# Norms of a Hymba-style decoder step: the reciprocal root as one power on GpSimd, spread over the partitions by ones times diagonals

## The chip, the cores and the metric

The kernel runs on one core of one Trainium2 chip. The metric is the device time of one launch in microseconds (us). Engines are named as in the profile: PE is TensorE's matmul, PEld its weight load, DVE is VectorE, ACT is ScalarE, POOL is GpSimd, SP is SyncE, which issues most DMAs; SPq, POOLq and ACTq are their DMA queues. All arithmetic is float32. A tile of type `fp32r` holds float32 values that were rounded so that PE reads them in one pass; a plain float32 matmul takes two passes of PE (two matmul records each). Where the kernel wants float32 accuracy from the rounded type it splits a value into a high part (the value, rounded) and a low part (the rest), and adds two or three products.

## The reference, cut to what matters

One layer of a decoder is computed for 2048 new tokens (the prompt) and for 8 x 4 = 32 sample tokens, 2080 columns in all. Width is 1024, the feed-forward width 2816.

```python
def rmsnorm(x, g):
    y = x32 * lax.rsqrt(jnp.mean(x32 * x32, axis=-1, keepdims=True) + EPS)   # EPS = 1e-6
    return y * g

a = rmsnorm(x, norm_attn_g)
qa, fa, ia, ga, qb, kb, vb = split(a @ w_in)
o_a = rmsnorm(gla_chunked(q_a, k_a, v_a, log(forget), s0), hgrn_onorm_g) * silu(ga)   # per head, 128 wide
o_b = dilated_attn(q_b, k_b, v_b)
h = x + concat(o_a, o_b) @ w_o
hn = rmsnorm(h, norm_ffn_g)
h = h + (silu(conv(hn @ w_gate)) * (hn @ w_up)) @ w_down
h = h + sigmoid(rmsnorm(h, norm_ple_g) @ w_ple_gate) * (p @ w_ple_proj)
y = rmsnorm(h, norm_final_g)
```

So a token is normed five times, and each norm needs one number for a token, 1/sqrt(mean + EPS).

## The kernel before, in words

Activations lie with features on partitions and tokens along the free dimension. A norm therefore needs a sum over partitions and then the result on every partition. It is made in these steps:

- `rstd_cols`: PE multiplies the tile of squares `ssq` by a column of ones, 128 tokens at a time (L114), so that 128 tokens stand on 128 partitions and a norm over T tokens is a tile of 128 x ceil(T/128) numbers, `rs_v`. DVE scales and adds EPS (L121, L122).
- `rsqrt_small`: DVE takes the reciprocal root of that small tile, by a bit trick on integers (L100, L101) and three Newton steps of three instructions (L103, L104, L105): 11 instructions that each need the one before.
- `bcast_rows`: for every column of 128 tokens, PE multiplies the column, repeated 128 times as weights, by the identity `ident` (L129). That leaves each token's number on all 128 partitions, in PSUM. These are float32 matmuls, two passes each. `bcast_all` does so for four columns at a time, and ACT copies the result to SBUF (L138).

The program has four parts.

1. Projections of the first 1024 and then of the other 1056 tokens (`in_phase`, norms at L254 on chunks of 256 to 384 tokens). Next to the first half, `w_down` is combined and rounded for a Strassen product and written to DRAM. A projection's output is scaled with the token's norm `rb` when DVE empties PSUM (L300), or with the column `rc` or `rq` by ACT (L357).
2. Next to the second half, eight units of the HGRN recurrence (`hgrn_unit`). Each norms its output per head: sums of squares by ACT (L558), `o_v` (L561), `rsqrt_small` on 128 x 8 (L562), then DVE scales `at` (L567), PE turns it (L574) and DVE gates it (`hg`, L575).
3. Attention over the prompt. On PE the order of this part is written out by hand (the scheduler may not move its matmuls). Into it are woven the last HGRN unit, the attention of the sample tokens, whose cached keys and values are loaded as `skt`, and the recurrence of the sample tokens, which has one norm of its own (`hsv`, L660 and L661, scaled at L662, turned at L665). POOL takes part in the attention: keys and queries are prepared there (`kL`, `qS`), and the coefficients of the three dilations.
4. The trunk: three blocks of 696, 696 and 688 tokens, first through the output product (`out_block`), then all through the feed-forward (`ffn_block`), then all through the embedding gate (`embed_block`). The product of the Strassen scheme with `w_down` (`downs`) is done there too; its weights `w` come from DRAM `wd_d` by DMAs that POOL issues (L1275). There are eight norms of whole blocks: three before the feed-forward, three before the gate, and the final norms of blocks 0 and 1. Two more make the final norm of block 2 (`now`, in 432 and 256 tokens). The steps of a norm are not done at once: `rstd` hands back two functions, one for the sums and the root, one for the spreading, and they are called some matmuls apart, as `mid` inside `dense_first` or from the list `late`.

Outside of the attention on PE, a scheduler orders the instructions of every engine, by a model of its own of how long things take; each engine then works through its list in that order. So a change in one place can move instructions in others. The pool of wide tiles of the trunk, `w` from `wide`, has 44 buffers.

## Time and profile before

| what | value |
|---|---|
| median of 3 runs | 3017.25 us (3016.31 to 3018.32) |
| the profiled execution | 3014.84 us |
| its span, first to last instruction | 3013.0 us |
| granted TensorE clock, mean | 0.988 |
| PE busy | 2926.5 us, 97% of the span |
| DVE busy | 2191.6 us, 73% |
| ACT busy | 1304.5 us, 43% |
| POOL busy | 667.9 us, 22% |
| `rsqrt_small` | 25 calls, 275 instructions on DVE |
| spreading matmuls (L129) | 71, in 142 records |

The profiled execution took 2.4 us less than the median. An engine's busy time is the time in which it works on anything; matmuls overlap, so that PE can be busy without being at its peak. A row of a timeline gives the start in us, the length in us, engine, line, operation and out<-in, and in brackets how long the engine sat idle before it and what ended that. Rows of equal neighbours are merged (x4).

### The profile page before, as it was taken

How to read it: one execution, taken by the hardware profiler on the slowest of the kernel's cores; microseconds unless marked ns; L12 is line 12 of the kernel's file. 1: busy time of each engine (PE TensorE's matmuls, PEld its weight loads, DVE VectorE, ACT ScalarE, POOL GpSimd, SP SyncE). 2: the span in 40 equal slices, each digit the busy share in tenths (PEclk: the TensorE clock that was granted, in tenths of full speed). 3: DMA queues.
4: the chain of work that ended last, by engine and by line, in shares of the span. 5: the costliest groups of instructions: out<-in, count | busy, mean ns of one | idle time of the engine just before them, and what ended most of it. 6: DMA issues, size and time to landing. Idle time of an engine off the chain costs nothing.

```text
span 3013.0 us, 52001 instructions
## 1 busy us (share of the span) xinstructions
PE 2926.5 (97%) x18639; PEld 2738.0 (91%) x18639; DVE 2191.6 (73%) x4761; ACT 1304.5 (43%) x2824; POOL 667.9 (22%) x780
## 2 busy tenths in 40 slices
PE   8999999999978989999999999999999999999998
PEld 8977789987767667999999999999999999999997
DVE  7666868884466557568988889766769777777777
ACT  5333423231156665334444444544444544444443
POOL 1443222221134553102443431000001000000000
PEclk9999999999989999999999999999999999999999
DMA  5898533342248996766666568677778777778873
GB/s 174 311 337 309 198 103 110 104 134 95 91 115 243 303 246 194 260 225 222 227 209 194 191 198 300 231 250 252 245 231 311 242 245 244 257 248 290 272 274 131
DMA packets 328579, 664.08 MB, mean 220 GB/s; under 512 B 46400, under 2 KB 114112, under 8 KB 326528
## 3 DMA queue, kind: packets, MB, share of 16 engines
q1 hardware_dynamic: 291472, 472.65, 48.4%
q0 software_dynamic: 33264, 121.13, 12.6%
q10 hardware_dynamic: 3584, 66.98, 6.1%
q8 instruction: 147, 2.41, 0.3%
q14 instruction: 112, 0.92, 0.1%
HBM read 513.69 MB, written 213.92 MB: 241 GB/s over the span
## 4 chain that ended last, share of the span: by engine, by line
PE 72%; issue 9%; DVE 7%; DMA 7%; ACT 2%; POOL 2%; SPq 1%; DVEq 0%; POOLq 0%; ACTq 0%
PE mm L142 16%; PE mm L144 16%; PE mm L143 16%; PE mm L346 2%; PE mm L344 2%; PE mm L345 2%; PE lv L484 2%; PE acc L822 2%; PE S L797 1%; PE PT L810 1%; PE S L798 1%; DMA draw<-in_w_down_dram 1%; DMA xr<-in_xT_dram 1%; DVE h L1291 1%; DMA wd_d<-dw 1%
## 5 line engine op out<-in xcount | busy, mean ns | idle before, releaser
L143 PE MATMUL mm<-w 128*128 128x348 f32 (+3 forms) x3636 | 1166.1, 321 | 1.1 <-DVE w L1435 0.7
L142 PE MATMUL mm<-w 128*128 128x348 f32 (+3 forms) x3508 | 1109.7, 323 | 15.2 <-ACT s L1233 5.8
L144 PE MATMUL mm<-w 128*128 128x348 f32 (+3 forms) x3508 | 1117.4, 321 | 1.3 <-DVE w L181 1.3
L143 PEld LDWEIGHTS mm<-w 128*128 128x128 f32 x3636 | 684.3, 188 | 3.8 <-DVE w L1067 1.8
L142 PEld LDWEIGHTS mm<-w 128*128 128x128 f32 x3508 | 656.5, 188 | 23.6 <-ACT s L1233 8.5
L144 PEld LDWEIGHTS mm<-w 128*128 128x128 f32 x3508 | 659.0, 188 | 2.6 <-DVE w L181 1.8
L181 DVE TENSOR_TENSOR w<-raw,w 128x512 fp32r<-128x512 f32 x586 | 421.9, 725 | 170.3 <-ACT w L180 165.3
L180 ACT CAST w<-raw 128x512 fp32r<-128x512 f32 x586 | 360.6, 621 | 402.8 <-PE mm L144 293.1
L1275 POOL DMA_DIRECT2D w<-wd_d x231 | 123.8, 536 | 906.2 <-PE mm L144 800.6
L1291 DVE TENSOR_TENSOR h<-h,mm 128x348 f32<-128x348 f32 (+1 forms) x504 | 248.4, 509 | 45.9 <-PE mm L144 44.4
L803 ACT ACTIVATE P<-P,st 128x256 f32<-128x256 f32 (+3 forms) x256 | 134.1, 526 | 87.5 <-DVE st L802 85.9
L802 DVE CUSTOM_DVE_ANT_0 P<-S,mask 128x256 f32<-128x256 f32 (+3 forms) x256 | 105.0, 449 | 73.1 <-PE S L798 50.1
L1233 ACT COPY s<-mm 128x348 f32<-128x348 f32 (+1 forms) x198 | 87.9, 444 | 158.1 <-PE mm L144 157.8
L345 PE MATMUL mm<-wl,xh 128*128 128x512 f32 x352 | 140.7, 400 | 1.1 <-DVE wl L267 1.1
L344 PE MATMUL mm<-wh,xh 128*128 128x512 f32 x352 | 140.6, 403 | 0.0
L346 PE MATMUL mm<-wh,xl 128*128 128x512 f32 x352 | 140.3, 399 | 0.0
L142 PE MATMUL mm<-xh,wh 128*128 128x384 f32 (+2 forms) x384 | 125.7, 332 | 8.6 <-ACT xh L242 5.1
L143 PE MATMUL mm<-xl,wh 128*128 128x384 f32 (+2 forms) x384 | 126.9, 333 | 0.8 <-DVE xl L243 0.8
L144 PE MATMUL mm<-xh,wl 128*128 128x384 f32 (+2 forms) x384 | 125.5, 330 | 1.5 <-DVE wl L267 1.4
L267 DVE TENSOR_TENSOR wl<-wraw,wh 128x512 fp32r<-128x512 f32 x104 | 86.3, 851 | 34.0 <-POOL wh L148 28.9
L181 DVE TENSOR_TENSOR dw<-draw,dw 128x512 fp32r<-128x512 f32 x77 | 69.4, 909 | 55.8 <-ACT dw L180 55.0
L797 PE MATMUL S<-kH,qS 128*128 128x256 f32 (+3 forms) x256 | 97.7, 396 | 8.2 <-DVE st L802 7.3
(348 smaller groups left out, 5155.0 us busy)
## 6 DMA issues: line engine op xcount, KB each, us to landing
w<-wd_d POOLq DMA_DIRECT2D x231, 512.0 KB, 5.6
wd_d<-dw SPq DMA_DIRECT2D x77, 512.0 KB
out_sk_dram<-in_cache_k_dram ACTq DMA_DIRECT2D x56, 584.0 KB
out_sv_dram<-in_cache_v_dram ACTq DMA_DIRECT2D x56, 584.0 KB
raw<-in_w_gate_dram SPq DMA_DIRECT2D x110, 256.0 KB
raw<-in_w_up_dram SPq DMA_DIRECT2D x110, 256.0 KB
wraw<-in_w_in_dram SPq DMA_DIRECT2D x104, 256.0 KB
raw<-w_gate_d SPq DMA_DIRECT2D x88, 256.0 KB
```

Of the source, the lines that this page charges most:

```text
L142: PE.matmul(ps, lhsT=wh, rhs=xh, start=first, stop=False, skip_group_check=read)
L143: PE.matmul(ps, lhsT=wh, rhs=xl, start=False, stop=False, skip_group_check=read)
L144: PE.matmul(ps, lhsT=wl, rhs=xh, start=False, stop=last, skip_group_check=read)
L180: A.copy(w[:, 0], raw)
L181: V.tensor_sub(w[:, 1], raw, f32(w[:, 0]))
L344: PE.matmul(ps, lhsT=xh[k][:, js], rhs=wh, start=k == 0, stop=False)
L345: PE.matmul(ps, lhsT=xh[k][:, js], rhs=wl, start=False, stop=False)
L346: PE.matmul(ps, lhsT=xl[k][:, js], rhs=wh, start=False, stop=k == NK - 1)
L797: PE.matmul(s[:, w * i:w * i + w], lhsT=bl.q(hh), rhs=bl.k(kH, hh), start=True, stop=False)
L803: A.activation(pe, pe, AF.Exp, bias=mn, scale=-1.0, accum_out=st[:, bl.r, hh, 0:1])
L1275: G.dma_start(t, wd_d[p][n - 1])
L1291: V.tensor_add(o, o, acc[m][:, :H])
```

## The change: what it does

- `rsqrt_small` becomes one instruction on POOL: the tile to the power of -0.5, the exponent read from a constant 128 x 1 tile. This holds for all 25 calls.
- For the eight whole-block norms of the trunk, `bcast_split` replaces `bcast_all`. The column of roots is split into `rs_hi` (rounded) and `rs_lo` (the rest) on DVE. For each group of up to four columns, a 128 x 512 tile is filled with the identity, times the column, so that each 128 x 128 block has 128 tokens' numbers on its diagonal: POOL makes the one of the high part, DVE the one of the low part, into two more buffers of the pool of wide tiles. PE multiplies each by a matrix of ones, both into the same PSUM tile, with the rounded type. The copy by ACT stays.
- The norms in `in_phase` and in `now` keep the old spreading.
- The old tile of ones shrinks to two columns; a rounded 128 x 128 tile of ones comes beside it.

```diff
-    ones = const.tile([128, 128], F32, name="ones")
+    ones = const.tile([128, 2], F32, name="ones")
     V.memset(ones, 1.0)
+    ones_r = const.tile([128, 128], F32R, name="ones_r")
+    V.tensor_copy(ones_r, ones[:, 0:1].to_broadcast([128, 128]))
+    power = const.tile([128, 1], F32, name="power")
+    G.memset(power, -0.5)
...
     def rsqrt_small(pool, v, shape):
-        i = pool.tile(shape, I32, name="rs_i")
         y = pool.tile(shape, F32, name="rs_y")
-        t = pool.tile(shape, F32, name="rs_t")
-        V.tensor_scalar(i, v.bitcast(I32), 1, None, op0=ALU.logical_shift_right)
-        V.tensor_scalar(y.bitcast(I32), i, -1.0, RSQRT_SEED, op0=ALU.mult, op1=ALU.add)
-        for _ in range(3):
-            V.tensor_mul(t, y, y)
-            V.scalar_tensor_tensor(t, t, -0.5, v, op0=ALU.mult, op1=ALU.mult)
-            V.scalar_tensor_tensor(y, t, 1.5, y, op0=ALU.add, op1=ALU.mult)
+        G.tensor_tensor(y, v, power.to_broadcast(shape), op=ALU.pow)
         return y
...
+    def bcast_split(pool, wide, pps, cols, nt, T, dst, tag="ms"):
+
+        hi = pool.tile([128, nt], F32R, name="rs_hi")
+        lo = pool.tile([128, nt], F32R, name="rs_lo")
+        V.tensor_copy(hi, cols)
+        V.tensor_sub(lo, cols, f32(hi))
+        for j0 in range(0, nt, 4):
+            nj = min(4, nt - j0)
+            n = min(T, 128 * (j0 + nj)) - 128 * j0
+            eye = ident.rearrange("p (o t) -> p o t", o=1).to_broadcast([128, nj, 128])
+            ps = pps.tile([128, 512], F32, name=tag)
+            for x, (part, eng) in enumerate(((hi, G), (lo, V))):
+                d = wide(128 * nj, F32R)
+                col = f32(part)[:, j0:j0 + nj].rearrange("p (j o) -> p j o", o=1).to_broadcast([128, nj, 128])
+                eng.tensor_mul(d.rearrange("p (j t) -> p j t", t=128), eye, col)
+                PE.matmul(ps[:, :n], lhsT=ones_r, rhs=d[:, :n],
+                          start=x == 0, stop=x == 1)
+            A.copy(dst[:, 128 * j0:128 * j0 + n], ps[:, :n])
...
-        def rstd(ssq, T, c0=0, n=None):
+        def rstd(ssq, T, c0=0, n=None, split=True):
...
-                        lambda: bcast_all(pmm, rc[0], -(-n // 128), n, rb[:, c0:c0 + n], "mm"))
+                        lambda: (bcast_split if split else bcast_all)(*([sm, wide] if split else []), pmm, rc[0], -(-n // 128), n,
+                                                                  rb[:, c0:c0 + n], "mm"))
 
         def now(ssq, T, c0=0, n=None):
-            rb, steps = rstd(ssq, T, c0, n)
+            rb, steps = rstd(ssq, T, c0, n, False)
```

A source line of the changed kernel stands 15 or 16 lines lower from `bcast_all` on (L567 becomes L582, L802 L817, L1291 L1307), and `rsqrt_small`'s power is L101, the diagonals and their matmuls are L143 and L144.

Three places of the order that the engines' lists show. First, the last HGRN unit, inside the attention: DVE before, up to the scaling of `at`. `rs_t` and `rs_y` are the root's steps, `pt` copies of turned scores, `mn` a minimum for the attention's coefficients, `hg` the gated output:

```order
L812 COPY pt<-PT 128x512
L736 TENSOR_REDUCE mn<-st 128x8
L104 SCALAR_TENSOR_TENSOR rs_t<-rs_t,o_v 128x8
L105 SCALAR_TENSOR_TENSOR rs_y<-rs_t,rs_y 128x8
L103 TENSOR_TENSOR rs_t<-rs_y 128x8
L567 TENSOR_TENSOR at<-at,rs_y 128x512 x2
```

These are the last rows of a stretch that begins with `o_v` (L561): between it and L567 stand the root's eleven steps, six scores (L802), three copies `pt` (as one, one and one) and `mn`, mixed. DVE in the changed kernel at the same place:

```order
L576 TENSOR_SCALAR o_v<-o_ssq 128x8
L817 ISA P,st<-S,mask 128x256
L827 COPY pt<-PT 128x512
L827 COPY pt<-PT 128x512 x2
L751 TENSOR_REDUCE mn<-st 128x8
L582 TENSOR_TENSOR at<-at,rs_y 128x512 x2
```

(The score row comes six times.) The eleven steps are gone; the same scores and copies stay ahead of the scaling. The power is POOL's, in the midst of its work for the attention:

```order
L752 TENSOR_TENSOR w<-mn,st 128x16
L711 TENSOR_TENSOR kL<-stage,kH 128x4x128
L101 TENSOR_TENSOR rs_y<-o_v,power 128x8
L163 TENSOR_SCALAR qS<-stage 128x512 x2
L755 TENSOR_TENSOR wl<-w,st 128x16
```

It stands between the two `kL`, which follow each other before.

Second, the first of the gate's norms (block 0), where the last products of the feed-forward are still being added to `h` (L1291 before, L1307 now) and weights are split (L181, now L196). DVE before:

```order
L122 TENSOR_SCALAR rs_v<-mm 128x5
L1291 TENSOR_TENSOR h<-h,mm 128x344 x2
L100 TENSOR_SCALAR rs_i<-rs_v 128x6
L181 TENSOR_TENSOR w<-raw,w 128x512
L101 TENSOR_SCALAR rs_y<-rs_i 128x6
L103 TENSOR_TENSOR rs_t<-rs_y 128x6
```

and DVE in the changed kernel:

```order
L118 TENSOR_SCALAR rs_v<-mm 128x5
L1307 TENSOR_TENSOR h<-h,mm 128x344 x2
L196 TENSOR_TENSOR w<-raw,w 128x512
L133 CAST rs_hi<-rs_y 128x6
L116 MEMSET rs_v 128x6
L1307 TENSOR_TENSOR h<-h,mm 128x344
L134 TENSOR_TENSOR rs_lo<-rs_y,rs_hi 128x6
L143 TENSOR_TENSOR w<-c_ident,rs_lo 128x512
L1307 TENSOR_TENSOR h<-h,mm 128x344 x4
L143 TENSOR_TENSOR w<-c_ident,rs_lo 128x256
```

(L1307 x2 comes once more ahead of the CAST, and L196 and L1307 once more ahead of the first L143.) Two small steps and two products of 512 and 256 elements have taken the place of ten small steps, and the CAST waits for POOL.

Third, PE in the trunk. Between a norm's sums (L114, now L110) and its first spreading matmul the scheduler puts other matmuls. For the eight norms in order their number was 49, 50, 60, 93, 44, 72, 41 and 24; now it is 79, 81, 36, 27, 41, 96, 43 and 24. At the fourth, the gate's first norm, PE in the changed kernel, from the first spreading matmul (high part) to the second (low part); L157 to L159 are the three products of `mm3`, 344 tokens wide:

```order
L144 MATMUL mm<-w,ones_r 128x512
L157 MATMUL mm<-w 128x344
L158 MATMUL mm<-w 128x344
L159 MATMUL mm<-w 128x344
L144 MATMUL mm<-w,ones_r 128x512
```

Where one block of twelve passes stood (L129 x6), there are now four single passes, here three to nine other matmuls apart, so that PE can wait at four places.

More of the change, by code (lines that the diff above doesn't have):

```diff
@@ L29 @@
 BIG = 1e30
-RSQRT_SEED = float(0x5F3759DF)
 BLOCKS = ((0, 1024), (1024, 1056))
```

## The prediction

> **What bounds the kernel now.** I read the page's shares first, then the stages, then who PE waits for, then the rows around each of the 25 roots.
>
> ```profile
> PE 2926.5 (97%) x18639; PEld 2738.0 (91%) x18639; DVE 2191.6 (73%) x4761; ACT 1304.5 (43%) x2824; POOL 667.9 (22%) x780
> ```
>
> ```profile
> core 0: us, PE busy (x) PEld busy (x) DVE busy (x) ACT busy (x) POOL busy (x), PEclk, DMA share, GB/s
> 420.00:840.00 420.00, 414.63 (x2483) 367.61 (x2482) 286.29 (x823) 98.87 (x268) 94.26 (x113) 0.99 0.35 112
> 930.00:1060.00 130.00, 122.97 (x1058) 89.10 (x1053) 72.66 (x273) 84.30 (x254) 57.89 (x69) 0.97 1.04 297
> 1240.00:1380.00 140.00, 140.00 (x900) 139.94 (x899) 92.37 (x159) 51.11 (x81) 4.76 (x4) 1.00 0.73 253
> 1380.00:1500.00 120.00, 115.77 (x717) 113.84 (x716) 115.69 (x171) 64.62 (x118) 47.01 (x34) 0.99 0.61 210
> 1500.00:2280.00 780.00, 776.40 (x4860) 773.16 (x4859) 605.60 (x1021) 349.91 (x672) 166.75 (x196) 1.00 0.71 233
> 2280.00:2745.00 465.00, 460.09 (x2899) 456.64 (x2899) 356.95 (x694) 226.09 (x473) 44.45 (x84) 1.00 0.78 258
> ```
>
> PE is the bound nearly everywhere: 140.0 of 140 us at the trunk's start, 414.6 of 420 next to HGRN. So DVE work that goes away is worth nothing by itself (275 steps of some 0.16 us, 44 us, 1.5% of the span); it counts only where PE waits at a root, or where PE itself has less to do. A matmul of the trunk costs 140.0 / 900 = 0.156 us.
>
> **The change, part by part.**
>
> *The tail.* The last norm stands alone on the path:
>
> ```profile
> 3001.84 0.16 DVE L122 TENSOR_SCALAR rs_v<-mm 128x2 f32<-128x2 f32 x1 [0.70 <-PE mm L114]
> 3002.03 0.17 DVE L100 TENSOR_SCALAR rs_i<-rs_v 128x2 int32<-128x2 int32 x1
> ...
> 3004.01 0.16 DVE L105 SCALAR_TENSOR_TENSOR rs_y<-rs_t,rs_y 128x2 f32<-128x2 f32 x1
> 3004.22 1.22 PE L129 MATMUL mm<-c_ident,rs_y 128*128 128x128 f32 x4 [2.42 <-DVE rs_y L105]
> ```
>
> Eleven steps from 3002.03 to 3004.17, and PE 0.05 us later: 2.2 us from `rs_v` to PE. In their place come a hop to POOL, one power and a hop to PE. No row has a power. The nearest, POOL's smallest two-input instruction:
>
> ```profile
> L741 POOL TENSOR_TENSOR mn<-wl 128x8 f32<-128x8 f32 x16 | 3.2, 201 | 0.9
> L696 POOL TENSOR_TENSOR kL<-stage,kH 128x512 fp32r<-128x512 f32 x30 | 46.0, 1552 | 12.7 <-ACT kH L695 10.8 <-issue 1.9
> ```
>
> It takes 0.20 us with as many elements; a power is more arithmetic. Bounds: 0.20 below; above 1.55, POOL's product of 64 times as many elements. I take 0.4, near the lower end, since most of 0.20 us cannot be arithmetic on 8 elements a partition. With two hops of 0.1 that is 0.6 for 2.2: -1.6 us (-1.8 to -0.45).
>
> *The start.* The first chunk's root is worked off in 9 us, since DVE weaves it into loading x:
>
> ```profile
> 21.67 0.15 DVE L122 TENSOR_SCALAR rs_v<-ms 128x2 f32<-128x2 f32 x1
> 31.24 0.15 DVE L105 SCALAR_TENSOR_TENSOR rs_y<-rs_t,rs_y 128x2 f32<-128x2 f32 x1
> 33.71 0.35 ACT L138 COPY rb<-ms 128x256 f32<-128x256 f32 x1
> 34.97 0.44 PE L142 MATMUL mm<-xh,wh 128*128 128x384 f32 x1 [2.25 <-DVE ev L300]
> ```
>
> PE has all its PSUM tiles full and waits 2.25 us for evictions that need `rb`. POOL is free there; with a root at 22.5 `rb` comes long before 31, and the wait goes. What is late next is x (ACT and its loads), so I take -2.0 (-2.3 to 0). The other five roots of the projections end no wait of PE: 0, covered by PE's 414.6 of 420 us and the like; were the cover gone, each would give back at most such a wait. The seven HGRN roots next to the projections likewise: 0, with 3 us either way for a reordered PE.
>
> *The last HGRN unit.* Here PE's order is fixed, and DVE is late:
>
> ```profile
> 911.15 0.50 DVE L561 TENSOR_SCALAR o_v<-o_ssq 128x8 f32<-128x8 f32 x1
> 911.88 3.07 POOL L696 TENSOR_TENSOR kL<-stage,kH 128x512 fp32r<-128x512 f32 x2
> 913.52 1.47 DVE L101 TENSOR_SCALAR rs_y<-rs_i 128x8 int32<-128x8 int32 x1
> 915.46 0.88 PE L822 MATMUL acc<-pt,v 128*64 128x128 f32 x12
> 920.69 1.29 DVE L567 TENSOR_TENSOR at<-at,rs_y 128x512 f32<-128x512 f32 x2
> 921.44 1.12 PE L574 MATMUL s<-c_ident,at 128*128 128x128 f32 x4 [5.10 <-DVE at L567]
> ```
>
> The root spreads over 9.5 us; one of its steps takes 1.47 us beside POOL's `kL`. Of the 9.5, some 4.9 are `o_v`, scores and copies that stay. The power stands behind the first `kL`, 911.88 + 3.07 / 2 = 913.4, and is done by 914: DVE no longer waits for it when it reaches L567 at about 916 to 917. PE, done at 916.3, then waits 0 to 1 us for 5.1. The wait costs more than its length:
>
> ```profile
> 916.00:922.00 6.00, 0.90 (x11) 0.66 (x6) 5.82 (x21) 2.25 (x9) 4.12 (x7) 0.81 0.86 213
> 922.00:926.00 4.00, 4.00 (x21) 3.67 (x21) 3.24 (x13) 3.19 (x7) 1.96 (x4) 0.50 0.76 266
> ```
>
> After it the granted clock is 0.50 for 4 us, that is 2 us of work. So 4.1 + 2 = 6 here. Behind it lies the loading of the sample's keys (DMA share 1.04 from 930 to 1060), which starts when this unit ends and so moves too, but not for certain. I take -4.5 (-7.2 to 0).
>
> *The sample's norm.*
>
> ```profile
> PE s L665 <- DVE hso L662: 1.5, 1, 1.5
> ```
>
> The same pattern, POOL idle: -1.2 (-1.5 to 0).
>
> *The trunk, PE's own work.* Eight spreadings of twelve passes become four passes each:
>
> ```profile
> 1290.52 1.21 PE mm L114 x12
> 1299.71 1.34 PE mm L129 x12
> ```
>
> ```profile
> 199.80 0.40 PE L345 MATMUL mm<-wl,xh 128*128 128x512 f32 x1
> 201.19 0.39 PE L345 MATMUL mm<-wl,xh 128*128 128x512 f32 x1
> ```
>
> The first pair is of the chain, start and share: 1.34 us for twelve. The second is a run of one-pass matmuls 512 wide: six in 1.39 us, 0.232 each. One of 184 lies between a 2-wide one (1.21 / 12 = 0.10) and a 344-wide one (0.156): 0.11. New: 2 x 0.232 + 2 x 0.11 = 0.68. Gain 0.66 x 8 = -5.2 us (-5.3 to -4.6).
>
> *The trunk, new waits.* From the sums to PE it is now DVE, POOL, DVE, POOL and DVE side by side. The diagonals are two-input products of 512 and 256 elements. POOL's:
>
> ```profile
> 1359.23 1.28 POOL L168 TENSOR_TENSOR raw<-raw 128x512 f32<-128x512 f32 x1 [133.02 <-DMA h_d<-h]
> 1445.77 1.28 POOL L176 TENSOR_TENSOR raw<-raw 128x512 f32<-128x512 f32 x1 [4.46 <-DVE rs_t L104]
> 1445.78 1.29 DVE L105 SCALAR_TENSOR_TENSOR rs_y<-rs_t,rs_y 128x6 f32<-128x6 f32 x1
> ```
>
> 1.28 us, and a DVE step beside it that else takes 0.16 takes 1.29: each POOL product can hold DVE as long. DVE has room for that (357 of 465 us) except at the trunk's feed-forward start (115.7 of 120). The chain, at the gate's first norm:
>
> ```profile
> 2746.88 1.47 PE L114 MATMUL mm<-ones,w 128*128 128x2 f32 x12 [0.70 <-DVE w L1048]
> 2747.59 0.68 DVE L181 TENSOR_TENSOR w<-raw,w 128x512 fp32r<-128x512 f32 x1
> 2749.03 0.14 DVE L121 TENSOR_SCALAR rs_v<-mm 56x1 f32<-56x1 f32 x1
> 2749.17 0.94 DVE L1291 TENSOR_TENSOR h<-h,mm 128x344 f32<-128x344 f32 x2
> ```
>
> Sums end at 2748.35; `rs_v` starts 0.68 later and takes 0.2; hop and power 0.5, hop and rounding 0.3, POOL's product 1.3: 3.0 us. Ahead of the rounding stand four additions (0.47 each) and a split (0.68), 2.6 us, of which 0.6 passes while POOL works: 5.0 in all. PE has 27 matmuls for it, 27 x 0.156 = 4.2. So PE is short 0.8, and as much again for the low part, whose product stands behind another split and two additions. By the same count the others have 12.3, 12.6, 5.6, 6.4, 15.0, 43 x 0.194 = 8.3 and 24 x 0.194 = 4.7 us (0.156 scaled to 432 columns); only the last is as tight. POOL's queue holds no DMA that would be late there: it is idle for 235 us from 2742 on.
>
> ```profile
> 2977.78 1.38 POOL L1513 TENSOR_SCALAR w<-w,c_gains 128x256 f32<-128x256 f32 x2 [235.22 <-ACT w L1044]
> ```
>
> For the first three it shares POOL with the weights' sums, with 5.6 us and more. I take +2.5 (0 to +8, a microsecond a norm). The four more wide buffers of a norm I cost at nothing: 44 cover them; if not, a load of `h` is late once a block, which the +8 holds.
>
> *Sum:* -1.6 - 2.0 - 4.5 - 1.2 - 5.2 + 2.5 = -12.0. Adding the ends gives -18 to +3 apart from the reordering. The profiled execution took 3014.84 and its span 3013.0, so 1.8 us lie outside and stay: 3002.8 for such an execution. The runs' median is 3017.25, 2.4 above it, and I forecast on that scale: 3017.25 - 12.0 = 3005.
>
> **The rivals.**
>
> *The gains outside the trunk aren't kept.* For: DMA share 1.04 right behind the largest of them; a stage that waits for loads gives nothing for an earlier start. Against: those loads are let go by the same unit's end, and PE is busy 123.0 of 130 us. Price: without -4.5, -1.2 and half of -2.0 the sum is -5.3: 3012.
>
> *PE waits in the trunk at every norm.* For: four places to wait instead of one, and the low part's product far down DVE's list. Against: six of eight norms have 5.6 us or more. Price: +8 for +2.5: 3010.5.
>
> *The power is slow* (the other side). POOL's row tells nothing of a power's arithmetic. Should it take 4.7 us, three times POOL's slowest row, the chain in the trunk is 9.3 us: short by 5.1, 4.6, 3.7, 2.9 and 1.0 at the five tight norms, 17.3 in all, and DVE stands still meanwhile at the rounding; -5.2 + 17.3 + 0.6 for the low part = +13. The tail loses 2.7, the unit in the attention gains only 2.5, the start still 2: +11, 3028. It decides from about 2.8 us a power on, where the trunk's loss (some +6) and a tail of +0.8 eat the rest. The Trainium skill (GPSIMD Engine Reference, Instruction dispatch) says that the first call into freshly loaded code of this engine pays about 6 us with no instruction to be seen. If the power lay in other code than the sums and were loaded at each change, the same working with 6 us would give about +20; no run here shows such a load.
>
> *The scheduler's new order costs.* PE's list differs in hundreds of rows from 300 to 840 us; 5.4 us of PE idle there can grow as well as shrink. Price 3 either way.
>
> **How the numbers follow.** A measurement here tells 0.2%, 6.0 us, from no change. The forecast, with sums from -8 to -17: 0.55, all faster. Gains not kept: 0.19, all within 0.2% (-5.3). Waits at every norm: 0.10, near -6.7, half faster and half within 0.2%. Slow power: 0.10, all slower. A costly order: 0.06, of which 0.04 within 0.2% and 0.02 slower. Faster 0.55 + 0.05 = 0.60; same 0.19 + 0.05 + 0.04 = 0.28; slower 0.10 + 0.02 = 0.12. The range runs from 3000 (-17) to 3018: below it 0.07, above it the slow power and part of the order, 0.12. The forecast's own range is 3000 to 3009.
>
> **What would show it.** A power below 0.5 us in POOL's rows; no wait of L574's successor at about 915 and a clock of 1.0 behind it; the first eviction before 31 us; four one-pass matmuls for each trunk norm, about 0.7 us; waits for POOL's and DVE's diagonals of 0 to 2 us at the gate's first and last norms; 0.6 us from `rs_v` to PE at the end. Powers above 2 us, or waits of PE for `w` of L143 beyond 5 us together, would prove it wrong.

## The result and the profile after

Eight runs of the changed kernel took 3029.16 us in the median, eight of the kernel before 3017.78; the ratio is 1.0038, 95% interval 1.0025 to 1.0052. So the change is slower, by 8 to 16 us, where -12 was forecast. The execution that was profiled first (8514.88 us, counted in that median; the other seven have 3026.78) is of no use for reading: rows of 348-wide matmuls are 0.66 us long in the mean there, where the next trace has 0.32, and a run of the kernel before took 7258.4 us later, so this is no matter of the change. The trace after is therefore that of another execution, 3032.50 us, on a chip where the changed kernel took 3028.98 in the median and the kernel before 3019.57, ratio 1.0027 (1.0014 to 1.0040). Line numbers of the changed kernel are 15 to 16 higher from `bcast_all` on: L567 is now L582, L574 is L589, L1141 is L1157; the new spreading is L133 (rounding), L134 (low part), L143 (diagonals) and L144 (PE), `mm3` is L157 to L159.

The page of the changed kernel, shares, and its windows with the columns of the windows shown before:

```profile
PE 2928.3 (97%) x18575; PEld 2738.5 (90%) x18575; DVE 2166.9 (71%) x4519; ACT 1304.1 (43%) x2824; POOL 707.6 (23%) x822
```

```profile
420.00:840.00 420.00, 412.19 (x2475) 366.74 (x2473) 273.82 (x738) 99.08 (x266) 106.63 (x120) 0.99 0.36 111
930.00:1060.00 130.00, 117.38 (x988) 82.76 (x986) 66.03 (x247) 77.38 (x236) 53.45 (x67) 0.95 1.03 274
1240.00:1380.00 140.00, 140.00 (x891) 139.77 (x890) 83.47 (x135) 50.30 (x78) 12.62 (x11) 1.00 0.69 239
1380.00:1500.00 120.00, 110.49 (x645) 105.63 (x644) 108.59 (x151) 58.18 (x108) 38.81 (x29) 0.94 0.65 225
2280.00:2745.00 465.00, 460.33 (x2904) 457.23 (x2903) 351.83 (x694) 219.45 (x467) 44.98 (x85) 1.00 0.78 260
```

DVE lost 25 us of work, as it should, and POOL gained 40. The window to look at is 1380 to 1500: PE did 645 matmuls there where it did 717, and its clock fell from 0.99 to 0.94, while DVE did less than before. PE is short of work, and DVE isn't the reason. Between 930 and 1060 PE is busy 5.6 us less; 3.1 us less are seen there in `before_b`, a second trace of the kernel before.

The power by shapes, in the groups of POOL (mean ns of one behind the busy time):

```profile
L101 POOL TENSOR_TENSOR rs_y<-o_v,power 128x8 f32<-128x8 f32 x8 | 13.3, 1659 | 6.0 <-DVE o_v L576 5.9
L101 POOL TENSOR_TENSOR rs_y<-rs_v,power 128x6 f32<-128x6 f32 x8 | 12.6, 1576 | 301.9 <-DVE rs_v L118 301.9
L101 POOL TENSOR_TENSOR rs_y<-rs_v,power 128x2 f32<-128x2 f32 x2 | 1.7, 834 | 6.0 <-DVE rs_v L118 6.0
L101 POOL TENSOR_TENSOR rs_y<-hsv,power 128x1 f32<-128x1 f32 x1 | 0.6, 571 | 5.6 <-DVE hsv L675 5.6
```

It costs by elements: 0.57 us for one on a partition, 1.66 for eight, which is four times the 0.4 I took. It is still less than the eleven steps it replaces, and below the 2.8 us from which I said it decides.

The second trunk norm, ahead of the second block's feed-forward, in the timeline of the changed kernel (start, duration, engine, line, operation; in brackets idle time and what ended it):

```profile
1362.02 1.36 PE L110 MATMUL mm<-ones,w 128*128 128x2 f32 x12
...
1364.45 1.35 POOL L101 TENSOR_TENSOR rs_y<-rs_v,power 128x6 f32<-128x6 f32 x1 [58.01 <-DVE rs_v L118]
1367.36 1.29 POOL L183 TENSOR_TENSOR raw<-raw 128x512 f32<-128x512 f32 x1 [1.56 <-DMA h_d<-h]
1368.73 1.28 POOL L187 TENSOR_TENSOR raw<-raw 128x512 f32<-128x512 f32 x1
1370.76 1.30 POOL L185 TENSOR_TENSOR raw<-raw 128x512 f32<-128x512 f32 x1 [0.74 <-DVE w L196]
1372.01 2.52 POOL L143 TENSOR_TENSOR w<-c_ident,rs_hi 128x512 fp32r<-128x512 f32 x2
...
1376.17 0.62 PE L144 MATMUL mm<-w,ones_r 128*128 128x512 f32 x2
1380.43 0.36 PE L144 MATMUL mm<-w,ones_r 128*128 128x184 f32 x2
...
1380.82 0.31 ACT L146 COPY w<-mm 128x184 f32<-128x184 f32 x1 [3.40 <-PE mm L144]
1381.17 6.93 DVE L1157 SCALAR_TENSOR_TENSOR w<-w,c_gains 128x696 f32<-128x696 f32 x8 [1.45 <-ACT w L146]
1382.14 6.30 SPq L1158 DMA_DIRECT2D hn_d<-w  x8
...
1389.71 0.42 SPq L1192 DMA_DIRECT2D w<-hn_d  x1
```

The root is there at 1365.8, but POOL's list puts three sums of weights ahead of the diagonals, PE's list puts 81 matmuls ahead of the first half of the spreading and 24 more ahead of the second, and `rb` is whole at 1381.1: 19.1 us after the sums began. Before, the same step took 11.2 us (sums at 1353.90, copies done at 1365.1, L1141 at 1365.22). The 31 matmuls more than before and the 24 between the halves, at 0.157 us each, are 8.6 of it.

Only with `rb` can DVE make the second block's normalised rows (L1157) and SP store them (L1158). What PE soon needs stands behind these eight stores in SP's list: the loads L1192 and L1194. By the kernel's text they fetch the rows of the first block, which were normed and stored long before, from 1319 us on; DVE and ACT prepare the Strassen sums of the first block's feed-forward from them. So PE does not wait for the rows that are normed here, but for a queue that they hold up. The loads start 27.7 us after the sums; with the power alone it is 20.3 us (sums at 1363.57, L1192 at 1383.91). The kernel before has the same order:

```profile
1366.18 6.82 SPq L1142 DMA_DIRECT2D hn_d<-w  x8
...
1374.88 0.43 SPq L1176 DMA_DIRECT2D w<-hn_d  x1
```

No run moves the loads ahead of the stores, so this link is read from the lists and not tried.

PE itself waits for nothing at L144; it pays later. Who PE waits for from 1362 to 1550, in three of six rows:

```profile
PE mm L157 <- ACT s L1249: 3.9, 3, 2.8
PE mm L157 <- ACT w L1082: 2.8, 2, 1.8
PE mm L157 <- ACT w L195: 1.9, 1, 1.9
```

L1082 and L1083 split the prepared rows in high and low parts. The loss stands in a stretch of 20 us, 48 us behind the sums. The changed kernel, the power alone, and `late_second` of the experiments:

```profile
1410.00:1430.00 20.00, 16.32 (x72) 14.09 (x71) 19.09 (x27) 11.60 (x19) 3.97 (x5) 0.74 0.47 146
```

```profile
1411.60:1431.60 20.00, 20.00 (x127) 19.77 (x126) 19.09 (x27) 16.13 (x29) 5.01 (x5) 1.00 0.42 139
```

```profile
1412.00:1432.00 20.00, 12.77 (x53) 10.76 (x52) 18.85 (x24) 11.22 (x19) 5.44 (x5) 0.74 0.50 160
```

The changed kernel does 72 matmuls there for 127, which at 0.157 us each is 8.7 us. Only 3.7 us of that is idle time of PE. The rest goes with its granted clock, 0.74 for 1.00. The prediction counted such a lower clock behind the wait in the last HGRN unit, and none behind a wait in the trunk.

### The profile page after: what moved, and what is told of

Same layout as the page of the kernel before. It is cut to its first block, busy times and chain, and to the rows that moved or that the text cites. A ratio compares the mean times of both kernels' runs of the same rounds, so it can differ in the third digit from the quotient of the medians.

```text
span 8513.1 us, 51704 instructions
## 1 busy us (share of the span) xinstructions
PE 8485.4 (100%) x18575; PEld 6355.2 (75%) x18575; DVE 2165.8 (25%) x4519; ACT 1319.8 (16%) x2824; POOL 673.7 (8%) x822
## 4 chain that ended last, share of the span: by engine, by line
PE 100%; issue 0%; DVE 0%; ACT 0%; DMA 0%; POOL 0%; DVEq 0%; SPq 0%; ACTq 0%; POOLq 0%
PE mm L157 21%; PE mm L158 21%; PE mm L159 21%; PE mm L360 3%; PE mm L359 3%; PE mm L361 3%; PE PT L825 3%; PE acc L837 3%; PE lv L499 2%; PE S L812 2%; PE S L813 1%; PE lv L359 1%; PE lv L360 1%; PE lv L361 1%; PE lv L157 1%; PE lv L159 1%
## 5 line engine op out<-in xcount | busy, mean ns | idle before, releaser
L158 PE MATMUL mm<-w 128*128 128x348 f32 (+3 forms) x3636 | 2410.1, 664 | 0.0
L159 PE MATMUL mm<-w 128*128 128x348 f32 (+3 forms) x3508 | 2314.8, 663 | 0.0
L157 PE MATMUL mm<-w 128*128 128x348 f32 (+3 forms) x3508 | 2297.2, 664 | 4.8 <-ACT s L1249 3.8
L158 PEld LDWEIGHTS mm<-w 128*128 128x128 f32 x3636 | 1340.4, 369 | 241.5 <-issue 143.5
L157 PEld LDWEIGHTS mm<-w 128*128 128x128 f32 x3508 | 1288.7, 368 | 246.4 <-issue 133.6
L159 PEld LDWEIGHTS mm<-w 128*128 128x128 f32 x3508 | 1291.9, 368 | 233.9 <-issue 138.5
L196 DVE TENSOR_TENSOR w<-raw,w 128x512 fp32r<-128x512 f32 x586 | 405.9, 695 | 1042.4 <-ACT w L195 1036.3
L1307 DVE TENSOR_TENSOR h<-h,mm 128x348 f32<-128x348 f32 (+1 forms) x504 | 259.8, 516 | 903.7 <-PE mm L159 903.1
L360 PE MATMUL mm<-wl,xh 128*128 128x512 f32 x352 | 391.1, 1114 | 0.0
L361 PE MATMUL mm<-wh,xl 128*128 128x512 f32 x352 | 388.4, 1106 | 0.0
L359 PE MATMUL mm<-wh,xh 128*128 128x512 f32 x352 | 388.2, 1109 | 0.0
L1291 POOL DMA_DIRECT2D w<-wd_d x231 | 123.7, 536 | 2753.5 <-PE mm L159 2753.5
L157 PE MATMUL mm<-xh,wh 128*128 128x384 f32 (+2 forms) x384 | 323.2, 848 | 5.1 <-ACT xh L257 5.1
L159 PE MATMUL mm<-xh,wl 128*128 128x384 f32 (+2 forms) x384 | 322.0, 845 | 0.0
L825 PE MATMUL PT<-c_ident,P 128*128 128x128 f32 x568 | 255.1, 696 | 0.0
L837 PE MATMUL acc<-pt,v 128*64 128x128 f32 x1136 | 236.5, 653 | 0.0
L499 PE MATMUL lv<-hM,hF 128*128 128x192 f32 x336 | 227.3, 905 | 0.0
```

The costliest lines, as they stand in the source:

```text
L157: PE.matmul(ps, lhsT=wh, rhs=xh, start=first, stop=False, skip_group_check=read)
L158: PE.matmul(ps, lhsT=wh, rhs=xl, start=False, stop=False, skip_group_check=read)
L159: PE.matmul(ps, lhsT=wl, rhs=xh, start=False, stop=last, skip_group_check=read)
L196: V.tensor_sub(w[:, 1], raw, f32(w[:, 0]))
L359: PE.matmul(ps, lhsT=xh[k][:, js], rhs=wh, start=k == 0, stop=False)
L360: PE.matmul(ps, lhsT=xh[k][:, js], rhs=wl, start=False, stop=False)
```

## The experiments

Each kernel was run in rounds beside the kernel before on the same chip (but `before_b` and `before_c`, one run each). "Power alone" means the power everywhere with the old spreading.

| kernel | ratio to before | 95% interval |
|---|---|---|
| `again` (the changed kernel) | 1.0027 | 1.0014 to 1.0040 |
| `power_only` | 0.9995 | 0.9982 to 1.0009 |
| `split_only` | 1.0045 | 1.0026 to 1.0064 |
| `power_early` | 1.0012 | 1.0000 to 1.0024 |
| `all_but_second` | 1.0020 | 1.0006 to 1.0033 |
| `second_only` | 1.0022 | 1.0011 to 1.0034 |
| `late_second` | 1.0047 | 1.0029 to 1.0065 |
| `trunk_power` | 1.0004 | 0.9992 to 1.0016 |
| `trunk_power_split` | 1.0002 | 0.9990 to 1.0014 |
| `newton_apart` | 1.0005 | 0.9993 to 1.0017 |
| `but_second_last` | 0.9987 | 0.9976 to 0.9999 |
| `trunk_power_b` | 0.9987 | 0.9976 to 0.9999 |
| `power_only_b` | 0.9991 | 0.9981 to 1.0000 |
| `four_buffers` | 1.0005 | 0.9991 to 1.0019 |

Single runs of one kernel lie up to 13 us from its median, so the place of a loss is read from the traces. The next table has eight numbers of each, in us, all starts of PE's instructions but `rb`: the first, 64th and last of the 128 key matmuls of the sample's attention (L928, now L943); the first sums of the trunk's first norm; from the second norm's sums to `rb` whole; from those sums to the 3000th L157 from the end; from the 200th to the 100th L157 from the end, where the eighth norm lies; and from the trunk's first sums to PE's end.

| trace | first key | 64th | last | trunk | `rb` 2nd | after 2nd | 8th | trunk to end |
|---|---|---|---|---|---|---|---|---|
| before | 939.1 | 970.2 | 1067.6 | 1290.4 | 11.2 | 178.6 | 64.8 | 1715.1 |
| `before_b` | 938.3 | 969.8 | 1072.6 | 1295.1 | 11.2 | 178.6 | 62.8 | 1710.6 |
| `before_c` | 937.6 | 968.7 | 1072.8 | 1296.6 | 11.2 | 177.1 | 64.1 | 1714.4 |
| `split_only` | 944.4 | 977.7 | 1079.5 | 1302.7 | 19.1 | 188.3 | 67.6 | 1724.1 |
| `power_early` | 936.3 | 973.2 | 1079.3 | 1304.0 | 11.2 | 178.6 | 65.1 | 1717.4 |
| `trunk_power` | 939.0 | 972.1 | 1070.8 | 1293.5 | 11.2 | 179.1 | 59.9 | 1707.4 |
| `trunk_power_b` | 938.7 | 972.1 | 1073.0 | 1293.2 | 11.2 | 179.1 | 59.9 | 1708.8 |
| `trunk_power_split` | 942.9 | 976.6 | 1076.1 | 1300.9 | 11.2 | 179.2 | 61.6 | 1710.5 |
| `newton_apart` | 939.4 | 977.1 | 1077.4 | 1298.6 | 11.2 | 181.1 | 59.9 | 1708.0 |
| `power_only` | 935.6 | 971.1 | 1076.7 | 1299.8 | 11.2 | 178.2 | 59.9 | 1707.1 |
| `power_only_b` | 934.1 | 971.0 | 1081.1 | 1301.9 | 11.2 | 181.1 | 59.9 | 1708.1 |
| `four_buffers` | 934.1 | 967.8 | 1075.6 | 1298.9 | 11.2 | 181.0 | 61.1 | 1708.3 |
| `again` | 934.3 | 970.3 | 1073.8 | 1299.0 | 19.1 | 188.3 | 66.0 | 1724.2 |
| `all_but_second` | 934.7 | 972.8 | 1076.5 | 1303.8 | 11.2 | 180.7 | 66.1 | 1713.3 |
| `but_second_last` | 936.6 | 972.4 | 1078.5 | 1301.5 | 11.2 | 182.7 | 60.3 | 1707.6 |
| `second_only` | 933.4 | 968.8 | 1071.5 | 1294.7 | 19.1 | 188.0 | 59.9 | 1714.6 |
| `late_second` | 934.6 | 971.8 | 1075.8 | 1300.3 | 22.5 | 189.5 | 60.0 | 1718.3 |

**The two halves of the change.** Four kernels: the change as it is; the power alone; the split spreading alone; and the power only before the trunk.

```
again           unchanged
power_only      def rstd(..., split=False)
split_only      rsqrt_small: the eleven DVE steps of before
power_early     split=False; rstd_cols: rsqrt_newton if tag == "mm" else rsqrt_small
```

> The changed kernel unaltered, for a trace in which PE runs at its usual speed (in the one at hand a 348-wide one-pass matmul takes 0.66 us, where the kernel before takes some 0.16). All theories: 3026 to 3032, 1.003 to 1.005 of before. They differ on where PE's 10 to 14 us are: theory T (trunk: waits for the diagonals, and loads late because four more wide buffers are taken at each norm) puts them behind 1240 us; theory E (early: the order that the scheduler makes with the power, and a power of 1.2 us and more instead of 0.4) puts them before 1240 us.

> Power everywhere, all norms spread by the identity as before. Theory T: the loss goes with the split spreading, so 3005 to 3015 (gains of start, attention and sample of 3 to 8 us kept). Theory E: the loss stays, 3025 to 3032.

> The eleven DVE steps kept, only the trunk's eight norms spread in high and low parts. Theory T: the loss stays or grows (DVE has more to do), 3022 to 3032. Theory E: no loss, 3011 to 3019 (PE's work of -5 against some waits).

> Power in the projections, the HGRN units and the sample's norm alone; in the trunk, its tail included, the eleven DVE steps and the old spreading. Theory T: 3007 to 3016. Theory E: 3025 to 3032 as with the power everywhere. Its difference to the power everywhere is what the power is worth in the trunk with the old spreading: by the prediction -1.6 at the tail and no wait, by a power of 1.2 us about -0.8.

The loss goes with the split spreading (1.0045 alone, 1.0027 with the power) and not with the power (0.9995), which is theory T in kind. In size it missed: `power_only` took 3017.62 us, above theory T's 3005 to 3015, and `split_only` 3035.61, above its 3022 to 3032. `power_early`, 3024.69 us where before took 3019.57, lies just below theory E's range and far above theory T's, so the power before the trunk brings no gain by itself. The traces say where the split's loss is: "after 2nd" is 188.3 us in both kernels with the split and 178.2 to 178.6 in before, `power_only` and `power_early`. The first 1240 us look unlike what I had forecast too, and that is taken up below.

**Is it the second norm, and is it `rb`?** Two kernels undo the split at that norm alone, or do it there alone.

```diff
 all_but_second
-                rb, (first, rows) = rstd(ssq, T)
+                rb, (first, rows) = rstd(ssq, T, split=b != 1)
 second_only     (split=False elsewhere)
+                rb, (first, rows) = rstd(ssq, T, split=b == 1)
```

> The changed kernel with the old spreading at one place: the second of the trunk's eight norms (the second block's, ahead of its feed-forward). Theory R (rb late): at that norm rb is ready 19.1 us after the sums instead of 11.2, so the products, the stores and loads of the normalised rows and the feed-forward's sums of inputs start 8 us later, and PE pays about 9 us for it between 1410 and 1500: here the waits there go, and the time is 3017 to 3022, within 3 us of the power alone. Theory B (buffers and DVE): all eight norms share the loss through the four more wide buffers and DVE's and POOL's products: 3026 to 3030, one to two us less than the changed kernel.

> The power everywhere, the split spreading at the second norm alone, the old spreading at the other seven. Theory R: 8 to 10 us above the power alone, 3025 to 3029, with rb ready some 19 us after the sums of the second norm and PE waiting between 1410 and 1500. Theory B: an eighth of the loss, 3017 to 3020.

(The second block's rows, of whose loads the first expectation speaks, are not the ones that are loaded there, as said above.) In the traces theory R holds on both sides: with the old spreading there "after 2nd" falls from 188.3 to 180.7, and the split there alone raises it to 188.0. In times the split at this one norm costs 8 us against the power alone (1.0022 and 0.9995 of about 3017, each to some 4 us). But `all_but_second` came out at 1.0020, not within 3 us of the power alone, so something else is lost: its "8th" is 66.1.

A late `rb` has been shown so far only together with its cause, the split. The next kernel makes `rb` late in another way:

```diff
+        for _ in range(late):            # 36 at the second norm, 0 elsewhere
+            G.tensor_tensor(y, y, ones[:, 0:1].to_broadcast([128, nt]), op=ALU.mult)
         return y
```

> The power everywhere and the old spreading everywhere; at the trunk's second norm alone 36 products with 1 of 128x6 on GpSimd (some 0.2 us each) stand between the power and the spreading, so that rb is some 7 us later, with nothing more on DVE, no more wide buffers and PE's own work as before. Theory R (rb late is enough): PE loses 6 to 10 us between 1410 and 1540, time 5 to 9 us above the power alone, 1.001 to 1.003 of before. Theory B (the loss comes from DVE's products and from the wide buffers): nothing, 0.999 to 1.0005.

In its timeline, POOL, then ACT; and who PE waits for, from 1364 to 1553:

```profile
1375.06 8.06 POOL L121 TENSOR_TENSOR rs_y<-rs_y,ones 128x6 f32<-128x6 f32 x26
...
1385.68 0.80 ACT L156 COPY w<-mm 128x512 f32<-128x512 f32 x2 [11.20 <-PE mm L128]
```

```profile
PE mm L160 <- ACT w L1085: 6.1, 2, 5.5
```

`rb` comes 22.5 us after the sums, 11.3 later than in the power alone (three sums of weights stand between the products), and "after 2nd" is 189.5. In the thirteen traces with `rb` at 11.2 us that column is 177.1 to 182.7, 179.6 in the mean; with the split there it is 188.0 to 188.3. So 7.9 us later cost about 8.6 and 11.3 later about 9.9. In the stretch of 20 us shown above `late_second` does 53 matmuls for 127, 11.7 us of work, of which 7.2 us are idle time of PE; its loads of the first block's rows start 31.0 us after the sums, 10.6 later than in the power alone. A late `rb` is enough for the loss, with no diagonal, no low part and no buffer more: theory B falls. The time, 1.0047, lies above theory R's own 1.001 to 1.003: `rb` is 11.3 us late there and not some 7. Against the power alone (0.9995 and 0.9991) the times say some 15 us and the traces 10 to 11 (1718.3 us from the trunk's start to the end for 1707.1 and 1708.1), which the intervals allow. (L1085 there is L1082; PE waits for no weight that POOL's products could have held up.)

The first norm is as late in the changed kernel (18.9 us for 11.3) and costs nothing to be seen: from its sums to the second norm's PE takes 63.0 us, before 63.5, and `all_but_second`, which keeps it late, has 180.7 behind the second. In SP's list loads of weights and of x stand behind its stores, and PE waits for nothing from 1300 to 1412 us.

**The eighth norm.** The final norm of block 1, the last of the eight. Its output is the result itself, and PE is at the embedding of the last block meanwhile.

```diff
 but_second_last (all_but_second, and)
-                rb2, (cols, rows) = rstd(ssq, T)
+                rb2, (cols, rows) = rstd(ssq, T, split=b != 1)
```

> The changed kernel with the old spreading at two places, the second and the eighth trunk norm. Theory E8 (the eighth norm holds what is left of the loss: between the sums of the seventh and the gains of the last block's output the split spreading takes 66 us where the power with the old spreading takes 60): 5 to 6 us below the kernel that keeps the split there, 0.9995 to 1.001 of before. Theory S (each split norm costs about a microsecond by its diagonals and buffers): 1.001 to 1.002, as with the one exception.

The "8th" column falls from 66.1 to 60.3, and the time from 1.0020 to 0.9987, below the expected 0.9995 to 1.001: E8 by the trace, with more in the time than the trace's 5.8 us. Both halves are at work here: the power with the old spreading at this norm takes 59.9 to 61.6 in nine traces, where the eleven steps take 62.8 to 65.1 in four, and the split gives that back. PE's waits there in the changed kernel (window 2949 to 2977), the queue of SP (2935 to 2972), and the window itself; then the window of the power alone that answers to it, in which PE waits for nothing:

```profile
PE mm L157 <- DVE w L1495: 2.1, 1, 2.1
PE mm L157 <- DVE w L1490: 1.8, 1, 1.8
```

```profile
SPq L1478 <- DVE w L1497: 6.8, 1, 6.8
```

```profile
2949.00:2977.00 28.00, 23.59 (x113) 21.34 (x112) 21.12 (x37) 9.37 (x18) 2.93 (x3) 0.88 0.67 230
```

```profile
2939.00:2961.00 22.00, 22.00 (x124) 21.08 (x123) 17.52 (x29) 7.59 (x15) 1.32 (x1) 1.00 0.80 290
```

SP's list stands 6.8 us at a load of `h` (L1478), which waits until DVE lets a buffer go; the embedding of the last block that needs it is late, PE waits 4.4 us in all, and the clock is 0.88 behind that. Is it the four more wide buffers? The identity was put in four of them, in the kernel with the power alone; the spreading's matmuls read it there:

```diff
+            eyes = [wide(512)[:, 0:128] for _ in range(4)]     # eighth norm alone
+            for d in eyes:
+                G.tensor_copy(d, ident)
```

> The power and the old spreading everywhere; at the eighth trunk norm alone the identity of the spreading is first copied by GpSimd into four buffers of the wide pool, which are held until the spreading. No rounding, no high and low parts, PE's work as before. Theory W (the four buffers make the load of h late, and with it the last block's embedding): SP waits 4 to 8 us at a load of h, PE takes 64 to 67 us from the 200th to the 100th matmul from the end (L157) instead of 60, time 1.0005 to 1.002 of before. Theory C (the longer chain through DVE and GpSimd does it): 60 us, and the time of the power alone, 0.999 to 1.0005.

The time tells nothing (1.0005 lies in both theories' ranges). The trace has 61.1 us, 1.2 above the power alone, and no such wait at SP: of the 6 us at the eighth norm the buffers alone explain about one, below theory W's 64 to 67. Theory W falls for the rest. That the split does it is shown; whether it is by the longer chain or by the changed order of loads and additions stays open.

**Before the trunk: where the power's gain goes.** These kernels tell it apart, and repeat two of them:

```
before_b, before_c   unchanged kernel before
newton_apart         power alone, but: r = (rsqrt_newton if apart else rsqrt_small)(...)
trunk_power          power and old spreading where tag == "mm", eleven DVE steps elsewhere
trunk_power_split    trunk_power, and: rb, steps = rstd(s.ssq, T, split=True)
trunk_power_b, power_only_b   once more
```

> The kernel before, unaltered, for a second trace of the stage with the sample's keys: from the first to the last of their 128 matmuls it took 128.5 us in the first trace of before, 135.1 to 143.0 in the four traces of kernels with parts of the change. Theory D (that stage is bound by its loads and scatters from run to run): 130 to 143 here too, with a time of 3015 to 3028. Theory P (the power itself slows the stage): 127 to 130.

> The kernel before once more, as a third trace of the same stage: theory D 130 to 143 us from the first to the last key matmul, theory P 127 to 130.

> The power everywhere, the old spreading everywhere, but the eleven DVE steps kept in the last HGRN unit (the one inside the attention). Theory L1 (it is this unit's earlier end that puts the attention and the sample's loads out of step): the stage from the first to the last key matmul is 128 to 136 us long again and the trunk starts 4 to 8 us earlier than with the power there, time 3 to 7 us below the power alone. Theory L2 (it is the earlier start of everything, some 3 us in the projections): the stage stays at 138 to 143 us, time as the power alone.

> The eleven DVE steps in the projections, the HGRN units and the sample's norm; the power in the trunk and its tail alone; the old spreading. Theory L (the early gains are taken back in the stage with the sample's loads, and the stage then gets some 5 us longer; from the first trunk norm on, the power gains 5 to 8 us): 4 to 7 us below before, 0.9975 to 0.999. Theory N (the differences before the trunk are scatter): about as the power everywhere, 0.999 to 1.0005.

> As the one ahead, and the split spreading at the gate's norms alone (the first of each block behind the feed-forward), where PE has other work while it waits and the normalised rows are needed late. Theory R: 0 to 2 us below the power in the trunk alone. Theory B: 2 to 4 us above it.

> The power in the trunk alone, the old spreading, a second time. Theory L (the trunk's 6 us are real, and what comes before is as in the kernel before): 0.9975 to 0.999 of before, and again some 1707 us from the first trunk norm's sums to the end, where the kernel before has 1711 to 1715. Theory N: 0.999 to 1.001.

> The power everywhere, the old spreading, a second time. Theory L: the early gain of some 4 us at the first key matmul is gone by the trunk, the first trunk norm 3 to 6 us later than in the kernel before, then 6 us gained: 0.999 to 1.0005. Theory N: the same time, but the first trunk norm anywhere within 1290 to 1304 us in both kernels.

What PE's key matmuls (L928, now L943) waited for, in the kernel before and with the power alone: first and last start in the first row of each, the waits in the second.

```profile
L928 PE MATMUL s<-skt,qb x128: 592/617/1059, 939.1 to 1067.6; 128*32 128x512 f32 x128
...
  DMA skt<-in_kT_d_dram: 10.8, 4
```

```profile
L943 PE MATMUL s<-skt,qb x128: 592/617/1061, 935.6 to 1076.7; 128*32 128x512 f32 x128
...
  DMA skt<-in_kT_d_dram: 26.8, 14
```

With the power in the HGRN units and the projections the first key matmul starts at 933.4 to 936.6 (nine traces), in the kernel before at 937.6 to 939.1 (three). At the 64th nothing is left of it: 967.8 to 973.2 and 968.7 to 970.2. The stage is held by its loads (DMA share 1.03), and an earlier start is only a longer wait for them. From there the traces part the other way: the last key matmul starts at 1071.5 to 1081.1 with the power and at 1067.6 to 1072.8 without, the trunk at 1294.7 to 1304.0 and 1290.4 to 1296.6. Theory D is right that the stage scatters by itself (128.5, 134.3 and 135.2 us in three traces of the same kernel), but not that scatter is all: the nine with the power are longer, 138.1 to 147.0. Three other kernels have the eleven steps ahead of this stage (`split_only`, `trunk_power` twice, `trunk_power_split`), and take 131.8 to 135.1. So seven traces without the power ahead of the stage and ten with it do not overlap; theory P's cause holds, though not its range. `newton_apart`, the tenth, does not start early and is 138.0 long, which neither L1 nor L2 explains. Why the stage gets longer is open.

In the trunk the power is worth 2 to 10 us by the traces: 1707.1 to 1708.8 from its first sums to the end in five traces with the power and the old spreading throughout the trunk (`trunk_power` and `power_only`, each twice, and `newton_apart`), 1710.6 to 1717.4 in the four with the eleven steps (the three of before, and `power_early`). In times `trunk_power` gave 1.0004 and 0.9987: theory L is not shown, nor excluded. The split at the three norms ahead of the gate adds nothing to be seen in the time (1.0002, and 1.0004 for `trunk_power` beside it, each to some 4 us). Its trace is 1.7 to 3.1 us longer from the trunk's start to the end than the two of `trunk_power`, so theory B's price is not excluded. The best kernels here, `but_second_last` and `trunk_power_b`, are 0.0001 to 0.0024 below before, and the second of them only in one of two goes; none clearly beats before.

## Why the prediction was wrong, point by point

- **The tail** (-1.6). Right, a little small: -1.4, since the power took 0.71 us where I took 0.4. `rs_v` to PE took 2.4 us from start to start and takes 1.0:

```profile
3021.05 0.16 DVE L118 TENSOR_SCALAR rs_v<-mm 128x2 f32<-128x2 f32 x1 [0.77 <-PE mm L110]
3021.29 0.71 POOL L101 TENSOR_TENSOR rs_y<-rs_v,power 128x2 f32<-128x2 f32 x1 [2.69 <-DVE rs_v L118]
3022.05 0.93 PEld L125 LDWEIGHTS mm<-c_ident,rs_y 128*128 128x128 f32 x4 [1.20 <-POOL rs_y L101]
```

- **The start** (-2.0). The mechanism was right: `rb` is copied at 25.95 where it was at 33.71, and PE no longer waits for an eviction there. The size was too small, and little of the gain lasts. The program's 61st matmul of L142 (now L157) starts at 37.3 to 38.5 us in five traces with the power there and at 42.4 to 44.6 in six without, some 5 us earlier. The 301st starts at 434.1 to 438.4 and 436.3 to 441.9, which overlap.

```profile
22.61 0.96 POOL L101 TENSOR_TENSOR rs_y<-rs_v,power 128x2 f32<-128x2 f32 x1 [3.36 <-DVE rs_v L118]
25.95 0.35 ACT L153 COPY rb<-ms 128x256 f32<-128x256 f32 x1
```

- **The last HGRN unit** (-4.5). The mechanism was right, the gain was not kept. The power stands behind the first `kL`, as said, `at` is scaled at once, and PE waits 0.8 for 5.1:

```profile
910.79 1.67 POOL L101 TENSOR_TENSOR rs_y<-o_v,power 128x8 f32<-128x8 f32 x1
913.70 1.84 DVE L582 TENSOR_TENSOR at<-at,rs_y 128x512 f32<-128x512 f32 x2
914.58 0.65 PE L589 MATMUL s<-c_ident,at 128*128 128x128 f32 x4 [0.80 <-DVE at L582]
```

  From the unit's last turns of `F` (L529) to its last turns of `o` PE takes 25.4 us for 32.0: -6.6. But the stage behind it is held by its loads, and at the 64th key matmul the gain is gone. This is the first rival, "the gains outside the trunk aren't kept". It came out worse than its price: not only the gain is lost, the stage behind gets longer.
- **The sample's norm** (-1.2). PE's wait of 1.5 us there is gone. What it is worth can't be seen behind a stage that differs by 7 us between traces of one kernel.
- **PE's own work in the trunk** (-5.2). Right in kind, a little small in size: at the second norm 0.62 + 0.36 = 0.98 us in place of 1.50, half a microsecond where I took 0.66. Over the eight norms it is an estimated -4.
- **The new waits** (+2.5, 0 to +8). This is the step that failed. I counted the matmuls between a norm's sums and its spreading and took them as cover: 79 and 81 at the first two norms, "12.3, 12.6" us. For PE they are cover: in the whole trunk it waits 0.3 us for a diagonal. For everything behind `rb` the same matmuls are delay. I asked how long PE waits for the norm, and never what stands behind PE's result in the other engines' lists. At the second norm the eight stores that need `rb` hold up the loads of the first block's rows by 7.4 us, and PE loses some 9 us to that, part as idle time and more than half as a lower clock. The eighth cost 6 more. So +15 at two places stood against +2.5 for eight. The profile before showed the order: L1176 right behind L1142 in SP's list. Of my signs of being wrong, the waits for L143 beyond 5 us did not come, since the loss lay elsewhere; one power above 2 us did come (2.06), and was not the reason.
- **Four more wide buffers** (nothing). By themselves about a microsecond at the eighth norm, though a load of `h` did stand there for 6.8.
- **The power** (0.4 us). 0.57 us for one element on a partition, some 1.65 for eight, and 1.32 to 2.07 for six. It didn't decide, though in the power alone PE waits for it at the third norm, where the scheduler now puts 24 matmuls ahead of the spreading for 60 before:

```profile
PE mm L125 <- POOL rs_y L101: 3.4, 1, 3.4
```

  The 6 us of code loading that I cited from the Trainium skill (GPSIMD Engine Reference, Instruction dispatch) don't show: the first power starts 0.08 us behind its operand and takes 0.96, and at the sample's norm and the tail it starts as close behind.

One sum in the prediction is off by a little: waits at every norm come to -12.0 - 2.5 + 8 = -6.5, or 3010.75, where it has 3010.5 and -6.7; no chance hangs on that.

The sum as it came out: from the trunk's first sums to the end the changed kernel takes 17.1 us more than the power alone (1724.2 and 1707.1), 10.1 of them behind the second norm and 6.1 at the eighth; the medians of the two on one chip differ by 11.4 (3028.98 and 3017.62). The power itself comes out at -1.5 (0.9995): by the traces a gain of some 6 in the trunk, and as much lost ahead of it, which the times can't part. Why the gains ahead of the trunk are lost stays open; the time that PE loses in the trunk is placed, at the eighth norm without its mechanism.

## What to carry to other kernels

Matmuls that a scheduler puts between a step and its result are cover only for the engine that does them. Where a small number (a norm, a scale) feeds stores or other work in an engine's list, look at what stands behind that work in the list, also where it does not read the number at all. Price a change by when that can start, and not by whether the busy engine waits at the step. Behind a wait of PE, count the lower clock too. And an earlier end ahead of a stage that is held by its loads is worth nothing until a trace shows the stage's own end to be earlier.

## What the runs showed that I had not expected

- A power on GpSimd costs by the element on a partition: 0.57 us for 1, 0.71 for 2, 1.09 for 4, 1.64 for 8, about 0.42 + 0.15 for each, where a product of the same 128x8 took 0.21 in the same trace (L756). For a norm's few columns it beats eleven dependent DVE steps of 0.16 to 0.2; by an estimate from these rates (0.15 an element against 2.0 us) the two meet at some ten columns.
- At the second norm PE loses about as much time as `rb` is late: 7.9 us late cost about 8.6, 11.3 late about 9.9, though PE is only 3.7 and 7.2 us idle there; in that stretch the granted clock is 0.74. At the first norm, 7.6 late cost nothing.
- The loads that PE was short of at the second norm bring rows of another block, by the kernel's text; in SP's list they stand behind this norm's stores.
- The sample's key stage takes 128.5 to 135.2 us in seven traces of four kernels without the power ahead of it, and 138.0 to 147.0 in ten traces of nine kernels with it. The cause is open.
